# Neighbourhood pairs prepared between the key projections, their bias tables loaded, streamed weights placed 192 bytes in, and adaLN steps of the second layer run two at a time

## The chip, the cores and the metric

The kernel runs on one core of one Trainium2 chip. The metric is the device time of one execution in microseconds (us). Four compute engines work from queues of their own, in order: PE (TensorE: matmuls, and transposes done as matmuls), DVE (VectorE), ACT (ScalarE) and POOL (GpSimd). SP issues the loads of weights. Operands of a matmul lie in the on-chip buffer (SBUF, 128 partitions), results go to accumulators (PSUM).

## The reference

Two layers over 512 latent tokens and 256 context tokens of 1024 features, everything in fp32. Each layer has a mixer and a convolution feed-forward block (FFN), each behind an RMS norm that is modulated by a conditioning vector (adaLN).

- adaLN: `silu(c) @ ada_w[l] + ada_b[l]`, 1024 x 6144 for each layer, split in six vectors of 1024 (shift, scale and gate for the mixer and for the FFN).
- Layer 0 mixer: a bidirectional mLSTM with 4 heads and windowed attention with 8 heads.
- Layer 1 mixer: global attention with 8 heads over all 768 keys, and neighbourhood attention with 8 heads. The latent tokens form a grid of 8 rows and 64 columns; a query sees 16 columns of all 8 rows and the 256 context keys. To its scores on grid keys a bias is added that depends on the head and on the distance in rows and columns, `rpb[h, dr, dc]`, and -1e30 for columns out of reach. Then follow the softmax, the product with the values, and the output projection `x + gate * (mix @ w_out)`.
- FFN: `(silu(gate) * val) @ w_down`, where gate and val are `conv3(h @ w_up)`, 1024 to 5632 and 2816 to 1024.

## The kernel before

**Products.** Each fp32 operand is split into a high part and the rest (names end in hi and lo, or h and l), and each product is the sum of three matmuls: high with high, rest with high, high with rest. In `mm3` (L179) the weights are held in PE and the tokens stream; in `gemm_set` (L329) a tile of 128 tokens is held and 256 columns of weights stream. The normed tokens stand in `hlh`, `hll` (512 latent) and `hch`, `hcl` (256 context), made by `htiles` (L308), which starts `hch` and `hcl` 192 bytes further in than a round address, `hlh` and `hll` at one.

**Weights.** `wchunk` (L153) loads 512 KB from DRAM into one of four buffers `raw`, issued by SP; ACT copies the high part to `whi` (L160), POOL subtracts it to get `wlo` (L161), each with three buffers. `whi` and `wlo` start at a round address.

**adaLN.** The matrix of a layer goes in three rounds (`ada_round`, L192). A round has eight steps of 1 MB: two loads into `raw` (L198) and four matmuls of 32 x 512 (L201), one on each quarter of PE's columns. The first two rounds of layer 0 run beside the mLSTM (all of layer 0's second one between 197 and 235 us). The three rounds of layer 1 are spread over the first FFN: `wchunk` counts a pace (`WP`) for each chunk of weights and lets a step go where the count is full.

**Stages.** Layer 0's mixer and projection end near 450 us, the first FFN runs to 1062, layer 1's projections and global attention to 1270, neighbourhood attention and half of the output projection to 1378, the rest of it and the second FFN to the end.

**Neighbourhood attention.** Heads are taken in four pairs. `prepD` (L974) prepares one: transposes of keys and queries on PE (L557, in `stacks`), the splitting into `T` and `L` parts on ACT, DVE and POOL, moves by DMA, and a bias table `E` (L987): 128 query positions by seven blocks of 256, six of them computed from a row of `rpb` loaded by DMA and a column mask `cmask`, three by DVE and three by POOL, and one set to zero (L980). Each pair then has four query tiles. For a tile and each of its two heads there are two score matmuls (L1026) into an accumulator `s`, the bias added and the smallest taken by one DVE instruction (L1029; the scores are negated, so it is the greatest), the Exp on ACT (L586), the reciprocal of the sum on DVE (L587), the division on POOL (L588), then transposes (L604), copies (L607, L609) and the value matmuls (L624). The outputs of global attention are split into `hlh` by ACT (L1002) and `hll` by POOL (L1003), in code ahead of the first pair; half of the output projection (L1051, its residual input `xcq` and `xnq` read from DRAM) is laid among the pairs.

**Order.** A scheduler that runs with a model of the engines puts the instructions of each engine in order when the kernel is built. The order of the code sets the priority, `pvs` raises that of the value matmuls, and each tile tag has a fixed number of buffers, whose release later users wait for.

## Time and profile before

| | |
|---|---|
| median of 3 runs | 1781.68 us (1780.98 to 1784.17) |
| profiled execution | 1781.26 us |
| its span, first to last instruction | 1779.5 us |
| mean granted clock of PE | 0.989 |
| PE busy | 1700.4 us, 96% |
| DVE, ACT, POOL busy | 47%, 37%, 38% |
| DMA, mean | 105 GB/s |

A row of a group of instructions gives line, engine, operation, output and inputs, then count, busy time, mean duration in ns, and the idle time of the engine ahead of them. Matmul records overlap: the end of one is modelled, so the distance from one start to the next is the time that it takes in a row of its kind. An fp32 matmul of 512 columns in `ada_round` leaves two records.

### The profile page before, as it was taken

The page shows a single profiled execution, that of the slowest core. Times are in us where ns is not written, and L with a number is a line of the kernel's source. Part 1 is how long each engine was busy: PE and PEld are TensorE (multiplying, and loading weights), DVE is VectorE, ACT ScalarE, POOL GpSimd, SP SyncE. Part 2 cuts the span into 40 slices and gives each one's busy share as a digit, 9 for nine tenths or more (in the row PEclk, how much of TensorE's full clock was granted, in tenths as well). Part 3 has the DMA queues.
Part 4 walks back from the last instruction along what each step waited for, and adds up shares of the span by engine and source line. Part 5 has one row for each costly group of instructions (what it writes and reads, how often), then busy time and mean ns, then how long its engine had stood idle before and what let it go on. Part 6 is the DMA issues. An engine that isn't in the chain of part 4 may idle for free.

```text
span 1779.5 us, 27798 instructions
## 1 busy us (share of the span) xinstructions
PE 1700.4 (96%) x11057; PEld 1458.8 (82%) x11057; DVE 837.8 (47%) x1904; ACT 656.8 (37%) x1139; POOL 676.9 (38%) x539
## 2 busy tenths in 40 slices
PE   5899998899999999999999999899989899999999
PEld 5679788789878888888888888799867888888887
DVE  5642458776653321333134356866266643143242
ACT  4422333544443311322133343365544453242341
POOL 2133226434422222222322363634474443444442
PEclk9999999999999999999999999999999999999999
DMA  8442431411322333333431251311342422322322
GB/s 317 169 169 71 155 136 48 131 31 36 107 95 83 131 107 131 107 127 101 139 131 55 67 194 53 84 40 28 84 128 69 154 94 85 107 92 87 106 88 78
DMA packets 62257, 187.62 MB, mean 105 GB/s; under 512 B 8048, under 2 KB 14320, under 8 KB 61872
## 3 DMA queue, kind: packets, MB, share of 16 engines
q1 hardware_dynamic: 62128, 185.85, 31.9%
q8 instruction: 87, 1.43, 0.3%
q14 instruction: 42, 0.34, 0.1%
HBM read 170.68 MB, written 4.39 MB: 98 GB/s over the span
## 4 chain that ended last, share of the span: by engine, by line
PE 81%; DVE 8%; issue 3%; ACT 3%; DMA 2%; POOL 2%; SPq 0%; POOLq 0%; ACTq 0%; DVEq 0%
PE s L185 11%; PE s L189 11%; PE s L187 11%; PE mm L185 4%; PE mm L187 3%; PE mm L189 3%; PE o L624 3%; PE t L185 3%; PE t L189 3%; PE t L187 3%; PE t L604 3%; PE mm L336 2%; PE o L185 2%; PE o L187 2%; PE o L189 2%
## 5 line engine op out<-in xcount | busy, mean ns | idle before, releaser
L161 POOL TENSOR_TENSOR wlo<-raw,whi 128x1024 fp32r<-128x1024 f32 (+3 forms) x210 | 485.7, 2318 | 850.1 <-ACT whi L160 815.5
L160 ACT ACTIVATE whi<-raw 128x1024 fp32r<-128x1024 f32 (+3 forms) x210 | 214.9, 1027 | 507.2 <-PE s L187 176.9
L185 PE MATMUL s<-hlh,whi 128*128 128x512 f32 (+1 forms) x696 | 272.9, 392 | 1.6 <-DVE cv L1124 1.0
L189 PE MATMUL s<-hlh,wlo 128*128 128x512 f32 (+1 forms) x696 | 271.0, 389 | 1.7 <-POOL wlo L161 1.7
L187 PE MATMUL s<-hll,whi 128*128 128x512 f32 (+1 forms) x696 | 271.3, 390 | 0.0
L1123 DVE SCALAR_TENSOR_TENSOR cv<-s,convw,cv 128x511 f32<-128x511 f32 x125 | 82.1, 657 | 318.3 <-ACT cv L1117 318.2
L185 PEld LDWEIGHTS s<-hlh,whi 128*128 128x128 f32 x696 | 131.1, 188 | 42.6 <-issue 13.4
L189 PEld LDWEIGHTS s<-hlh,wlo 128*128 128x128 f32 x696 | 131.1, 188 | 29.4 <-POOL wlo L161 2.1
L187 PEld LDWEIGHTS s<-hll,whi 128*128 128x128 f32 x696 | 131.0, 188 | 26.2 <-issue 0.8
L588 POOL TENSOR_SCALAR P<-P,sm 128x512 f32<-128x512 f32 (+3 forms) x112 | 84.3, 756 | 109.5 <-DVE sm L587 81.3
L185 PE MATMUL s<-hch,whi 128*128 128x256 f32 x376 | 106.4, 283 | 0.0
L187 PE MATMUL s<-hcl,whi 128*128 128x256 f32 x376 | 106.2, 282 | 0.0
L189 PE MATMUL s<-hch,wlo 128*128 128x256 f32 x376 | 106.1, 282 | 0.0
L336 PE MATMUL mm<-whi,hlh 128*128 128x256 f32 x320 | 94.3, 295 | 6.1 <-ACT l1xt L898 2.4
L337 PE MATMUL mm<-wlo,hlh 128*128 128x256 f32 x320 | 92.0, 288 | 0.0
L338 PE MATMUL mm<-whi,hll 128*128 128x256 f32 x320 | 91.9, 287 | 0.1
L604 PE MATMUL t<-ident,P 128*128 128x128 f32 x496 | 77.8, 278 | 9.6 <-POOL E L987 4.8
L1124 DVE SCALAR_TENSOR_TENSOR cv<-s,convw,cv 128x511 f32<-128x511 f32 x125 | 82.5, 660 | 4.3
L185 PE MATMUL t<-gh,whi 128*128 128x512 f32 (+1 forms) x213 | 82.1, 386 | 0.0
L189 PE MATMUL t<-gh,wlo 128*128 128x512 f32 (+1 forms) x213 | 81.4, 382 | 0.0
L187 PE MATMUL t<-gl,whi 128*128 128x512 f32 (+1 forms) x213 | 81.0, 381 | 0.0
L1163 ACT ACTIVATE gh<-cv 128x768 fp32r<-128x768 f32 (+1 forms) x44 | 32.5, 739 | 122.7 <-DVE cv L1162 122.7
(460 smaller groups left out, 4078.5 us busy)
## 6 DMA issues: line engine op xcount, KB each, us to landing
raw<-ada SPq DMA_DIRECT2D x96, 512.0 KB, 4.0
raw<-up SPq DMA_DIRECT2D x86, 512.0 KB, 3.6
raw<-down SPq DMA_DIRECT2D x40, 448.0 KB, 3.2
raw<-wout SPq DMA_DIRECT2D x24, 512.0 KB, 3.5
raw<-wodd SPq DMA_DIRECT2D x18, 512.0 KB, 3.7
raw<-down SPq DMA_DIRECT2D x16, 512.0 KB, 3.5
raw<-wtok SPq DMA_DIRECT2D x12, 512.0 KB, 3.8
raw<-wqk SPq DMA_DIRECT2D x8, 512.0 KB, 4.1
```

Of the source, the lines that this page charges most:

```text
L160: nc.scalar.activation(hi[:, :cols], raw[:, :cols], AF.Copy)
L161: nc.gpsimd.tensor_tensor(lo[:, :cols], raw[:, :cols], hi[:, :cols], op=ALU.subtract)
L185: nc.tensor.matmul(ps, wh, hh(k), start=(k == 0), stop=False, skip_group_check=True)
L187: nc.tensor.matmul(ps, wh, hl(k), start=False, stop=False, skip_group_check=True)
L189: nc.tensor.matmul(ps, wl, hh(k), start=False, stop=(k == nk - 1), skip_group_check=True)
L336: nc.tensor.matmul(ps[:, :ncols], a, W[k][0], start=(k == 0), stop=False, skip_group_check=True)
L337: nc.tensor.matmul(ps[:, :ncols], a, W[k][1], start=False, stop=False, skip_group_check=True)
L338: nc.tensor.matmul(ps[:, :ncols], b, W[k][0], start=False, stop=(k == KT - 1), skip_group_check=True)
L588: nc.gpsimd.tensor_scalar(Pt[:, :n], Pt[:, :n], sm, 0.0, op0=ALU.mult, op1=ALU.add)
L604: nc.tensor.transpose(tp[:, (b - g0) * P:(b - g0 + 1) * P], Pts[e][:, b * P:(b + 1) * P], self.ident)
L1123: nc.vector.scalar_tensor_tensor(y[:, a + 1:b], u[:, 0:n - 1], w(0), y[:, a + 1:b], op0=ALU.mult, op1=ALU.add)
L1124: nc.vector.scalar_tensor_tensor(y[:, a:b - 1], u[:, 1:n], w(2), y[:, a:b - 1], op0=ALU.mult, op1=ALU.add)
```

## The change

1. `ada_round` takes `run`. The three rounds of layer 1 use `run=2`: a step has four loads, into four buffers of its own (`rawa`), and eight matmuls; the pace falls from 0.55 to 0.28. In every step the first matmul now waits for all loads of the step.
2. `chunks` asks `wchunk` for `whi` and `wlo` that start 48 floats (192 bytes) into a buffer of 1088. Weights for `mm3` stay at the start of theirs.
3. Pairs 0 and 1 are prepared between the two halves of the key and query projections; four buffers of `stacks` are handed out in the order T, L, T, L.
4. The bias tables are laid out on the host and loaded by one DMA of 917 KB for a pair, into two buffers. The 24 additions, four zeroings, eight loads of `rpb` and the load of `cmask` go.
5. Both heads of a query tile share one accumulator `s` (1024 columns). The scores keep their sign, so the greatest is taken and negated by an instruction of DVE of its own.
6. The splitting of global attention's outputs stands behind the first pair in the code.

```diff
-PACE1, PACE, WP = 2.2, 2.5, 0.55
+PACE1, PACE, WP = 2.2, 2.5, 0.28
+SKEW = 48, 64
...
-        new = keep or (lambda tag: self.stg.tile([P, 1024], F32R, tag=tag, bufs=WH, name=self.n(tag)))
+        new = keep or (lambda tag: self.stg.tile([P, 1024 + SKEW[1]], F32R, tag=tag, bufs=WH, name=self.n(tag))[:, skew:skew + 1024])
...
+        ks = max(run, 1)
+        for k0 in range(0, KT, ks):
+            loads = []
+            for k in range(k0, k0 + ks):
+                for h in range(2):
+                    raw = pool.tile([P, 1024], F32, tag="rawa", bufs=2 * ks, name=self.n("raw")) if run else self.raw()
...
+                    if i == 0 and q == 0:
+                        for *_, name in loads[1:]:
+                            self.tc.add_manual_dep(m.ins, name, AFTER)
+            if k0 + ks < KT:
...
-            hi, lo = self.wchunk(blk[:, k0:k1, :].rearrange("p k c -> p (k c)"), (k1 - k0) * ncols, keep)
+            hi, lo = self.wchunk(blk[:, k0:k1, :].rearrange("p k c -> p (k c)"), (k1 - k0) * ncols, keep, SKEW[0])
...
+        both = [new() for _ in range(4 if swapped else 2)]
+        T = both[::2] if swapped else both
...
+            E = ap.tile([P, 7, 256], F32, tag="E", bufs=2, name=self.n("E"))
+            nc.sync.dma_start(E, d["bias"][p])
...
+            if b == 0:
+                ready = [prepD(0), prepD(1)]
...
+            if 0 < p < 3:
+                ready.append(prepD(p + 1))
...
+                both = self.psum("s")
                 for e in range(2):
-                    s = self.psum("s")
+                    s = both[:, 512 * e:512 * e + 512]
...
-                                                   scale=1.0, scalar=3.0e38, op0=ALU.add, op1=ALU.min, accum_out=mx)
-                    self.probs(ap, S, S[:, 0:512], mx, 512, sign=-1.0)
+                                                   scale=1.0, scalar=-3.0e38, op0=ALU.add, op1=ALU.max, accum_out=mx)
+                    nc.vector.tensor_scalar(mx, mx, -1.0, None, op0=ALU.mult)
+                    self.probs(ap, S, S[:, 0:512], mx, 512)
...
+            if p == 0:
+                for pc in range(4):
+                    v = lambda m: m[:, pc, :].rearrange("p (r t c) -> p r t c", t=4, c=16)
+                    src = oC[:, pc].rearrange("p t (c r) -> p r t c", r=8)
+                    nc.scalar.activation(v(M[0]), src, AF.Copy)
+                    nc.gpsimd.tensor_tensor(v(M[1]), src, v(M[0]), op=ALU.subtract)
...
-    later = [self.ada_round(1, r, self.nrm) for r in range(3)]
+    later = [self.ada_round(1, r, self.nrm, run=2) for r in range(3)]
```

How it moves instructions shows in three places. The first is PE beside the mLSTM of layer 0, in its second adaLN round (L201, accumulator `mm`). Lines 454, 464, 473 and 475 are the mLSTM's. Before:

```order
L464 MATMUL t_1559<-qk 128x128
L201 MATMUL mm_2437<-raw_2460,sc 32x512 x2
L473 MATMUL s_1544<-V,W_1540 128x129
L475 MATMUL s_1544<-C_1482,qk 128x129
L464 MATMUL t_1582<-qk 128x128
L473 MATMUL s_1523<-V,W_1519 128x129
L475 MATMUL s_1523<-C_1482,qk 128x129
L464 MATMUL t_1605<-qk 128x128
L201 MATMUL mm_2437<-raw_2464,sc 32x512 x2
L337 MATMUL o_2484<-wlo_2456,hlh_87 128x256
```

and now (L210 is the matmul of adaLN, L466, L476, L485 and L487 the mLSTM's):

```order
L476 MATMUL t_1559<-qk 128x128
L485 MATMUL s_1544<-V,W_1540 128x129
L487 MATMUL s_1544<-C_1482,qk 128x129
L476 MATMUL t_1582<-qk 128x128
L485 MATMUL s_1523<-V,W_1519 128x129
L487 MATMUL s_1523<-C_1482,qk 128x129
L476 MATMUL t_1605<-qk 128x128
L210 MATMUL mm_2437<-raw_2460,sc 32x512 x2
L210 MATMUL mm_2437<-raw_2462,sc 32x512 x2
L485 MATMUL s_1544<-V,W_1540 128x129
```

The two pieces of two matmuls of a step have become one piece of four; over the whole round, 12 pieces (the first of eight matmuls) have become 7. In the first FFN, 24 pieces of four become 12 of eight, one of which stands in three parts.

The second place is POOL where neighbourhood attention begins: `hll` is the rest of global attention's outputs, `P` the probabilities, `wlo` weights, `E` the bias table. Before:

```order
L1003 TENSOR_TENSOR hll_12643<-cq,hlh_12642 128x512 x4
L588 TENSOR_SCALAR P_12705<-P_12705,sm_12707 128x512
L588 TENSOR_SCALAR P_12715<-P_12715,sm_12717 128x512
L588 TENSOR_SCALAR P_12739<-P_12739,sm_12741 128x512
L588 TENSOR_SCALAR P_12749<-P_12749,sm_12751 128x512
L161 TENSOR_TENSOR wlo_13516<-raw_13514,whi_13515 128x1024
L980 MEMSET E_12690 128x256
L987 TENSOR_TENSOR E_12690<-adab,raw_12689 128x256 x3
L980 MEMSET E_13124 128x256
L987 TENSOR_TENSOR E_13124<-adab,raw_13123 128x256 x3
L588 TENSOR_SCALAR P_12789<-P_12789,sm_12791 128x512
```

and now (L584 and L586 are the copies of `stacks`, L601 the division of `P`, L1045 `hll`, L163 `wlo`):

```order
L601 TENSOR_SCALAR P_12678<-P_12678,sm_12681 128x512
L601 TENSOR_SCALAR P_12688<-P_12688,sm_12691 128x512
L601 TENSOR_SCALAR P_12713<-P_12713,sm_12716 128x512
L601 TENSOR_SCALAR P_12723<-P_12723,sm_12726 128x512
L1045 TENSOR_TENSOR hll_12670<-cq,hlh_12669 128x512 x4
L601 TENSOR_SCALAR P_12764<-P_12764,sm_12767 128x512
L601 TENSOR_SCALAR P_12774<-P_12774,sm_12777 128x512
L601 TENSOR_SCALAR P_12799<-P_12799,sm_12802 128x512
L163 TENSOR_TENSOR wlo_13495<-raw_13493,whi_13494 128x1024
L163 TENSOR_TENSOR wlo_13529<-raw_13527,whi_13528 128x1024
L601 TENSOR_SCALAR P_12809<-P_12809,sm_12812 128x512
```

The four instructions for `hll` stand behind four for `P`, and none for `E` is left. The transposes of pairs 0 and 1 stay, on PE, where they were, near the end of global attention.

The third place is PE at the preparation of pair 3: the transposes from `nq` are the last that read it, and `xnq` is loaded over it. L604 are transposes of `P`, L1026 scores, L624 value matmuls. Before:

```order
L1026 MATMUL s_13229<-K_12872,Q_12892 128x512
L557 MATMUL t_13110<-ident,nq 128x128 x4
L604 MATMUL t_13156<-ident,P_13139 128x128 x4
L604 MATMUL t_13163<-ident,P_13149 128x128 x4
L604 MATMUL t_13190<-ident,P_13173 128x128 x4
L1026 MATMUL s_13253<-K_12871,Q_12889 128x512
L1026 MATMUL s_13253<-K_12871,Q_12891 128x512
L604 MATMUL t_13197<-ident,P_13183 128x128 x4
L1026 MATMUL s_13263<-K_12872,Q_12890 128x512
L1026 MATMUL s_13263<-K_12872,Q_12892 128x512
L624 MATMUL o_13134<-PT_13155,l1xt 64x128
```

and now (L570 the transposes of `stacks`, L1024 scores, L617 transposes of `P`, L187 to L191 the output projection):

```order
L570 MATMUL t_13090<-ident,nq 128x128 x4
L1024 MATMUL s_13227<-K_12856,Q_12874 128x512
L1024 MATMUL s_13227<-K_12856,Q_12875 128x512
L617 MATMUL t_13128<-ident,P_13110 128x128 x4
L617 MATMUL t_13135<-ident,P_13120 128x128 x4
L617 MATMUL t_13163<-ident,P_13145 128x128 x4
L1024 MATMUL s_13192<-K_12857,Q_12876 128x512
L1024 MATMUL s_13192<-K_12857,Q_12877 128x512
L1024 MATMUL s_13227<-K_12857,Q_12876 128x512
L1024 MATMUL s_13227<-K_12857,Q_12877 128x512
L187 MATMUL mm_13547<-hlh_12669,whi_13528 128x512
```

Sixteen transposes of `P`, four score matmuls and the 16 value matmuls of two tiles stood between the transposes from `nq` and the next product of the output projection; now it is twelve and six, and the value matmuls stand behind a product.

## Rows read from the trace of the kernel before

**Rows 1.** Stretches: length, busy time of PE, PEld, DVE, ACT, POOL, clock, DMA, GB/s.

```profile
0.00:20.00 20.00, 4.45 (x42) 3.45 (x42) 8.11 (x33) 10.49 (x20) 7.68 (x20) 1.00 0.88 320
200.00:240.00 40.00, 39.08 (x254) 26.50 (x253) 16.23 (x65) 12.73 (x39) 9.42 (x6) 1.00 0.72 250
520.00:1000.00 480.00, 480.00 (x2809) 405.24 (x2808) 153.21 (x236) 125.54 (x134) 129.28 (x55) 1.00 0.32 108
1280.00:1300.00 20.00, 15.92 (x103) 13.03 (x101) 11.04 (x18) 10.46 (x18) 17.19 (x18) 1.00 0.66 181
1300.00:1320.00 20.00, 17.25 (x96) 14.17 (x97) 13.28 (x32) 8.43 (x18) 14.39 (x14) 0.83 0.39 128
```

**Rows 2.** Timeline of PE, an adaLN step in the FFN: start, length, instruction.

```profile
576.94 1.06 PE L201 MATMUL o<-raw,sc 128*32 128x512 f32 x8
577.94 0.50 PE L185 MATMUL s<-hlh,whi 128*128 128x512 f32 x1
578.28 0.40 PE L187 MATMUL s<-hll,whi 128*128 128x512 f32 x1
578.51 0.39 PE L189 MATMUL s<-hlh,wlo 128*128 128x512 f32 x1
```

**Rows 3.** Timeline of PE, layer 0, two adaLN steps in one piece.

```profile
196.90 1.92 PE L201 MATMUL mm<-raw,sc 128*32 128x512 f32 x16
198.75 0.49 PE L454 MATMUL t<-V,kw 128*128 128x129 f32 x2
```

**Rows 4.** Stretches, line 201 alone: length, busy time of PE and PEld, clock, DMA, GB/s.

```profile
198.90:232.90 34.00, 11.56 (x40) 1.57 (x40) 1.00 0.74 256
520.00:1000.00 480.00, 23.44 (x176) 3.46 (x176) 1.00 0.32 108
```

**Rows 5.** Loads of adaLN: timeline of SP's queue, and issue to landing in us.

```profile
509.71 2.70 SPq L198 DMA_DIRECT2D raw<-ada  x2
raw<-ada SPq DMA_DIRECT2D x96, 512.0 KB, 4.0
```

**Rows 6.** Groups of PE by form, `gemm_set` with latent and context tokens held.

```profile
L337 PE MATMUL mm<-wlo,hlh 128*128 128x256 f32 x320 | 92.0, 288 | 0.0
L337 PE MATMUL mm<-wlo,hch 128*128 128x256 f32 x112 | 31.6, 282 | 0.0
```

**Rows 7.** Chain of waits at the start of global attention: start, length, what.

```profile
1149.19 3.58 DVE E L987 x3
```

**Rows 8.** Chain of waits at the start of neighbourhood attention; timeline of PE there.

```profile
1282.70 1.21 ACT hlh L1002
...
1284.04 6.38 POOL hll L1003 x4
1290.42 1.24 POOL P L588 x2
...
1293.11 2.36 POOL wlo L161
...
1295.72 3.12 POOL E L987 x3
...
1302.26 1.09 PE L604 MATMUL t<-ident,P 128*128 128x128 f32 x4 [4.77 <-POOL E L987]
```

**Rows 9.** Chain of waits behind the transposes of pair 3; timeline of PE there.

```profile
1343.00 6.18 DMA xnq<-xd
...
1349.20 0.76 DVE xnq L1070
...
1347.89 1.09 PE L624 MATMUL o<-PT,l1xt 128*64 128x128 f32 x16 [0.52 <-ACT PT L609]
...
1350.01 0.50 PE L185 MATMUL mm<-hlh,whi 128*128 128x512 f32 x1 [0.15 <-DVE xnq L1070]
```

**Rows 10.** A small instruction of DVE in neighbourhood attention.

```profile
L587 DVE RECIPROCAL sm<-sm 128x1 f32<-128x1 f32 x32 | 5.1, 160 | 9.4 <-ACT P L586 9.2
```

More of the change, by code (lines that the diff above doesn't have):

```diff
@@ L550, in stacks @@
         new = lambda: pool.tile([P, n], F32R, tag=tag, bufs=bufs, name=self.n(tag))
-        T = [new(), new()]
-        L = [new(), new()] if swapped else [pool.tile([P, TOK], F32R, tag="stL", bufs=1, name=self.n("stL"))[:, :n]] * 2
+        both = [new() for _ in range(4 if swapped else 2)]
+        T = both[::2] if swapped else both
+        L = both[1::2] if swapped else [pool.tile([P, TOK], F32R, tag="stL", bufs=1, name=self.n("stL"))[:, :n]] * 2
         for g0 in range(0, nt, 4):
@@ L972, in odd_mixer @@
             self.qk_norm(ap, nq[:, :, c], NLT, 4, None, None, tmp)
-        def prepD(p):
-            ks = self.stacks(ap, nk, p * P, NTT, "K", False, bufs=4, g=nag[:, 1:2])
-            qs = self.stacks(ap, nq, p * P, NLT, "Q", True, bufs=8, rev=True, g=nag[:, 0:1])
-            raw = self.raw()
-            E = (self.res.tile([P, 8, 256], F32, tag=("hch", "hcl")[p // 2], name=self.n("E")) if p % 2 else
-                 ap.tile([P, 7, 256], F32, tag="E", bufs=1, name=self.n("E")))
-            nc.gpsimd.memset(E[:, 3], 0.0)
-            for e in range(2):
-                h = 2 * p + e
-                R = raw[:, e * 512:e * 512 + 265]
-                nc.sync.dma_start(R, bass.AP(tensor=rpb.tensor, offset=rpb.offset + 64 + h * 465 - 16, ap=[[1, 16], [31, 8], [1, 265]]))
-                for v in range(3):
-                    view = bass.AP(tensor=R.tensor, offset=R.offset + 16 - 8 * v, ap=[R.ap[0], [1, 32], [31, 8]])
-                    (nc.vector, nc.gpsimd)[e].tensor_tensor(E[:, 4 * e + v].rearrange("p (c r) -> p c r", r=8),
-                                                            cmask[:, v].unsqueeze(2).to_broadcast([P, 32, 8]), view, op=ALU.subtract)
-            return ks, qs, E
+            if b == 0:
+                ready = [prepD(0), prepD(1)]
         self.pve = 1
-        nxt = prepD(0)
         for b in range(2):
@@ L1300, in layout @@
     a["cos1"], a["sin1"] = tl(np.cos(ang)[cols]), tl((np.sin(ang) * sgn)[cols])
-    cq = (P - 1 - np.arange(P)) // 8
-    mask = []
-    for i, c0 in ((0, 0), (1, 8), (3, 32)):
-        ck = c0 + np.arange(32)
-        st = np.clip(16 * i + cq - 8, 0, 48)[:, None]
-        mask.append(np.where((ck >= st) & (ck < st + 16), 0.0, -NEG))
-    a["cmask"] = C(np.stack(mask, 1).astype(f))
+    q = P - 1 - np.arange(P)
+    rows = np.arange(8)[None, None, :] - (q % 8)[:, None, None] + 7
+    tabs = np.zeros((4, P, 7, 256), f)
+    for v, (i, c0) in enumerate(((0, 0), (1, 8), (3, 32))):
+        cq, ck = (16 * i + q // 8)[:, None, None], (c0 + np.arange(32))[None, :, None]
+        st = np.clip(cq - 8, 0, 48)
+        seen = (ck >= st) & (ck < st + 16)
+        idx = rows * 31 + np.clip(ck - cq + 15, 0, 30)
+        for h in range(8):
+            tabs[h // 2, :, 4 * (h % 2) + v] = np.where(seen, g["na_rpb"][0, h].reshape(-1)[idx], f(NEG)).reshape(P, 256)
+    a["bias"] = tabs
     for k, s in _SHAPES.items():
```

43 lines of the change are left out of this document (17 added, 26 removed).

## The prediction

> **What bounds the kernel now.** I read the stretches first. In the first FFN PE is busy for all of its 480 us at full clock, with DMA at 32% [rows 1]: there, only fewer or shorter instructions of PE save time, and any wait put on PE costs its full length. The second adaLN round of layer 0 is mixed, PE 39.08 of 40 us and DMA at 72% [rows 1]. Where neighbourhood attention starts (1280 to 1320) PE is idle for 4.08 + 2.75 us, and in the second half the granted clock is 0.83 [rows 1]. If the time below full clock was spent at 1.2 GHz, the lower of its two levels, 0.17 x 20 us = 3.4 us of work were lost to it too: some 10 us in all. Then the chain of waits, for what stands behind that idle time: it runs through ACT and POOL, `hlh`, `hll`, two `P`, a `wlo`, then the bias tables [rows 8]. Last, the timelines of PE around single adaLN steps, for the price of a step.
>
> **The sum, part by part.** It is made against the profiled execution, 1781.26 us (its span 1779.5 and 1.8 around it), which lies 0.4 us below the median of the runs.
>
> *adaLN in the first FFN.* One step of four matmuls takes 577.94 - 576.94 = 1.00 us, and the next matmul then takes 0.34 to the start of the one behind it, where the following one takes 0.23: 0.11 more [rows 2]. Two steps in one piece took 198.75 - 196.90 = 1.85 us [rows 3]. Twice 1.11 against 1.85 + 0.11 saves 0.26 a pair. Of the 12 pairs one stands in three parts, so 11 x 0.26 = -2.9 us. If only the 0.11 is saved, it is -1.2; if the trace's first piece hides some more, -4. The new wait of a piece's first matmul for four loads I cost at nothing: the stretch moves 108 GB/s [rows 1], a piece comes once in some 480 / 12 = 40 us, its four buffers are its own and free as soon as the piece before is done, and a load lands 4.0 us after its issue [rows 5]. What it costs without that cover is the third rival.
>
> *adaLN in layer 0.* After the first piece, 40 records, that is 20 matmuls in pieces of one or two, kept PE 11.56 us [rows 4]. Five steps in pieces of four cost 5 x 1.06 = 5.3 by the length of the step of [rows 2]: -6.3 us if PE alone sets the pace. But each piece now waits for both of its loads, and the round reads its megabytes through the four buffers that the other weights use too, at 256 GB/s [rows 4]; the highest rate that a row shows is 320 [rows 1]. The 12 adaLN loads and 3 of weights of that stretch are 7.9 MB, 25 us at that rate, of 34: loads can follow PE only in part. So 0 to -6.3, and I take the middle, -3.
>
> *Weights 192 bytes in.* In `gemm_set` the weights stand at a round address. With `hlh` held, at a round address too, the mean record is 288 ns; with `hch` held, which starts 192 bytes in, 282 [rows 6]. After the change the pairs are swapped: weights and latent tokens lie differently, weights and context tokens alike. If that is what makes the 6 ns, the 1392 matmuls with `hlh` or `hll` win and the 528 with `hch` or `hcl` lose (both counted over all groups of lines 336 to 338, of which [rows 6] show one each). Records overlap, a start following the last by 0.12 us, so I take 6/288 of 0.12, 2.5 ns each: 2.5 x (1392 - 528) = -2.2 us. Ends: 0, and with the whole 6 ns, -5.2.
>
> Against this part stands a rule of the Trainium skill, "TensorE: Matmul & The Clock Gate", in "Step-by-step: what each phase is for": PE reads the streamed operand and the next held operand through two independent ports, and "Loading the next tile's weights doesn't steal SBUF read bandwidth from the running matmul". By that rule the distance between two operands would not matter and the term would be 0. The rows with 288 and 282 ns speak against it, though weakly, as the ends of matmul records are modelled.
>
> *Bias tables.* At the start of global attention DVE spends 3.58 us on three of them in the chain of waits [rows 7], while score work waits behind it. It goes. Half of it will be lost to the next late thing, DVE's own queue of norms: -1.8, between 0 and -3.6. The loads of 0.9 MB that replace it go in stretches where DMA has room (66% at most, [rows 1]).
>
> *Start of neighbourhood attention.* Three things go from POOL's queue before the `P` that PE waits for: two memsets with their additions, 3.12 us for three [rows 8], and the four `hll`, 6.38 us [rows 8], which now stand behind the first four `P`. The 4.77 us that PE waited for the table [rows 8] goes, and the late first `P` (at 1290.42) comes some 6 us earlier. What is late next is the fifth `P`, behind `hll`; by then PE has the transposes, value matmuls and projections of two query tiles. Of the 10 us I count -8.
>
> Two things come back. Behind the transposes of pair 3, `xnq` is loaded in 6.18 us, and the product that needs it started 0.15 us after its release [rows 9]: before, the 16 value matmuls (1347.89 to 1350.01, 2.1 us) were part of its cover. They now stand behind that product, so PE waits for about 2 us more: +2. And DVE gets 32 negations of one column. The nearest row is the reciprocal of a column, 160 ns [rows 10]: 5.1 us of DVE in all, each between the maximum and the Exp. With two heads in flight most of it lies beside other work; I take +1, between 0 and +5.1. The shared accumulator `s` changes which scores may run ahead, not their number: 0, between -1 and +1. Together -8 + 2 + 1 = -5, between -10 and +1.
>
> That pairs 0 and 1 are prepared earlier in the code I cost at nothing: the order leaves their transposes where they were on PE.
>
> Sum: -2.9 - 3 - 2.2 - 1.8 - 5 = -14.9, so 1766.4 against the profiled execution, and 1767 with the 0.4 to the median.
>
> **The rivals.**
>
> *The gain at neighbourhood attention is given back.* The first `P` is early, but the negations sit in every chain from score to Exp, `hll` is late for the first product of the projection, and the wait for `xnq` drops the clock as the wait at 1302 did. Then the -5 becomes 0: 1772. For it speaks that PE's idle time between 1280 and 1380 has many releasers, so that removing one shows the next; against it, that POOL held 17.19 of 20 us there [rows 1] and loses 6 of them.
>
> *The offset does nothing*, by the skill's rule above or because the 6 ns belongs to the tokens alone. All else as forecast: 1769.
>
> *Slower: each piece of eight waits for its loads.* PE takes its queue in order, so a piece whose fourth load has not landed holds the whole FFN. SP issues four loads in a row behind weight loads, which wait for a buffer that POOL releases; two adaLN loads took its queue 2.70 us [rows 5]. One such time late at each of 12 pieces is 12 x 2.7 = +32, against -15: 1799. It decides from 15 / 12 = 1.2 us late a piece. Against it: in the order SP's four loads stand ahead of weights that PE uses after the piece, and the stretch leaves two thirds of DMA idle.
>
> *Nothing that counts.* The layer 0 round stays with its loads, the start of neighbourhood attention is set by ACT's Exps, pieces of eight save 1.2: 1779 or so.
>
> **How the numbers follow.** The forecast 45%, with a range of its own of 1760 to 1771; the gain given back 22%; no effect of the offset 13%; the slower one 10%; nothing that counts 10%. A measurement of this kernel tells some 0.2%, 3.6 us, from no change. Faster by more than that are the first three, 80%; within it the last and a weak form of the slower one, 11%; slower 9%. All ends of the terms at once would give 1781.3 - 4 - 6.3 - 5.2 - 3.6 - 10 = 1752, or 1781; half way to the first, and past no change at the other end, the range is 1757 to 1781, which leaves out the slower rival and a little below.
>
> **What would show it.** In the FFN, 12 pieces of 16 records with 1.85 us to the next start and no idle time ahead of them, PE still busy for all of 520 to 1000; a bracket with a DMA as releaser at those pieces proves the third rival. Between 199 and 235, six pieces of 8 records of about 1.06 us, and weight matmuls some 3 us earlier from there on; idle time of PE released by `raw<-ada` means the loads set the pace. The mean record of line 348 to 350 falls with `hlh` and rises with `hch`; if all stay, the offset does nothing. At the start of neighbourhood attention, no bracket of 4.77 us and a granted clock of 1.00; if PE waits for ACT's Exp or for `hll` by as much, the first rival holds. Behind pair 3's transposes, a wait for `xnq` of about 2 us.

## The result and the profile after

The changed kernel takes 1771.34 us (median of 6 runs, 1767.76 to 1775.91) against 1781.87 us of the kernel before (6 runs, 1780.06 to 1786.64): ratio 0.9939, 95% interval 0.9925 to 0.9952. It is faster, by 0.6% or 10.9 us; 1767 was forecast, with a range of 1757 to 1781. The profiled execution took 1767.76 us, with a span of 1766.0.

The runs of the changed kernel differ by 8 us (13 in one of the kernels below), and their mean granted clock differs with them (0.982 to 0.990 in the changed kernel). One of the twelve runs of skew_alone, below, was slow, at 3768.69 us, and is left out of its ratio. Two measures stand beside the ratio. One is where a given matmul starts in two traces. Of each kernel there is one trace, and kernels with the same code differ in it: by up to 4.9 us at the end of layer 0's second adaLN round, by about 1 us in how long the first FFN takes. The other is span times mean granted clock, averaged over the runs of a kernel: an estimate of the time at full clock. Its standard deviation over the runs of one kernel is 1 to 3 us, so that two means of six runs that are less than some 3 us apart can't be told apart by it.

Where the 13.5 us between the two traces come from (start of the same matmul, read from both traces):

| | before | after | difference |
|---|---|---|---|
| first matmul of `gemm_set`, behind the first adaLN round of layer 0 | 117.3 | 113.3 | -4.0 |
| first value matmul of windowed attention, behind the second round | 337.8 | 330.7 | -7.1 |
| first product of the first FFN | 486.5 | 479.0 | -7.5 |
| first projection of layer 1 | 1061.7 | 1054.6 | -7.1 |
| first score of global attention | 1138.3 | 1129.7 | -8.5 |
| last score of neighbourhood attention | 1368.8 | 1354.7 | -14.1 |
| first product of the second FFN | 1420.8 | 1408.4 | -12.4 |
| end of PE | 1776.3 | 1762.8 | -13.5 |

**adaLN.** The stretches of line 210 alone, as in [rows 4] (length, busy time of PE and of weight loads, clock, DMA, GB/s), of the changed kernel:

```profile
50.00:120.00 70.00, 8.33 (x64) 1.45 (x64) 0.98 0.58 192
195.00:231.00 36.00, 6.39 (x48) 0.97 (x48) 1.00 0.73 253
520.00:1000.00 480.00, 22.41 (x176) 4.62 (x176) 1.00 0.32 108
```

Between 195 and 231, 24 matmuls take 6.39 us where 20 took 11.56 [rows 4]: a piece of four takes 1.00 us to the start of what follows, where a piece of two or of one took 0.98. (The trace of the kernel before has 13 pieces in the second round, two of them of one matmul.) Over that round this is 7.9 us of pieces for 13.6. But PE now waits more among them. The round as a whole, all instructions, before and after (columns as in [rows 1]):

```profile
190.00:240.00 50.00, 48.92 (x334) 34.49 (x333) 21.26 (x84) 14.48 (x46) 10.90 (x7) 1.00 0.60 205
```

```profile
190.00:240.00 50.00, 45.69 (x362) 36.65 (x362) 26.06 (x79) 15.97 (x45) 15.70 (x9) 1.00 0.66 224
```

and PE's longest waits in it (who waits for whom: us in total, times, longest), before and after:

```profile
PE o L336 <- ACT whi L160: 0.8, 1, 0.8
```

```profile
PE o L348 <- DVE bq L760: 2.4, 1, 2.4
PE o L348 <- ACT whi L162: 1.1, 1, 1.1
```

Part of the matmul time that was saved has turned into waits for DVE and ACT (`bq` is a copy that frees an accumulator).

The FFN has 22.41 us for the same 176 records that took 23.44 [rows 4]. The timeline of PE in the first FFN (start, length, instruction, idle time before and its releaser), with the first piece and the wait that follows later:

```profile
484.02 1.92 PE L210 MATMUL o<-raw,sc 128*32 128x512 f32 x16
485.88 0.50 PE L187 MATMUL mm<-hlh,whi 128*128 128x512 f32 x1
...
510.99 0.77 PE L187 MATMUL s<-hlh,whi 128*128 128x512 f32 x1 [2.06 <-DVE cv L1129]
511.55 0.63 PE L189 MATMUL s<-hll,whi 128*128 128x512 f32 x1
511.98 0.63 PE L191 MATMUL s<-hlh,wlo 128*128 128x512 f32 x1
```

A piece of eight takes 1.86 us, as forecast, and none waits for its loads. But 25 us later PE waits 2.06 us for DVE, and the matmuls behind the wait take 0.56 and then 0.43 us to the next start instead of 0.23. The stretch it stands in (columns as in [rows 1]), changed kernel:

```profile
510.00:520.00 10.00, 9.01 (x40) 7.66 (x41) 5.04 (x8) 1.98 (x3) 0.00 (x0) 0.83 0.06 22
```

The granted clock is 0.83 there: it fell to 1.2 GHz behind the wait, which costs 0.17 x 10 = 1.7 us. The kernel before had a step of four just ahead of that place, a wait of 0.95 behind it, and no loss of clock:

```profile
515.54 1.19 PE L201 MATMUL o<-raw,sc 128*32 128x512 f32 x8
517.68 0.47 PE L185 MATMUL s<-hlh,whi 128*128 128x512 f32 x1 [0.95 <-DVE cv L1124]
```

```profile
510.00:520.00 10.00, 9.04 (x54) 7.13 (x53) 8.08 (x13) 6.00 (x7) 4.41 (x2) 1.00 0.65 225
```

**Streamed weights.** Rows of `gemm_set` in the changed kernel, to be held against [rows 6]:

```profile
L349 PE MATMUL mm<-wlo,hlh 128*128 128x256 f32 x320 | 91.1, 285 | 0.0
...
L349 PE MATMUL mm<-wlo,hch 128*128 128x256 f32 x112 | 31.9, 285 | 0.0
```

288 fell to 285 with latent tokens held and 282 rose to 285 with context tokens held. From one start to the next, over all pairs of neighbours without idle time between, the distance went from 119.5 to 115.6 ns (latent) and from 116.9 to 119.4 ns (context). The 115.6 is a mean of two spacings: of 1194 intervals 637 are 113 to 115 ns and 520 are 116 to 119, and a chunk of weights, twelve matmuls in a row, mostly has the one or the other. Two sets of twelve intervals (timeline of PE, first and last start), 1.36 us and 1.41:

```profile
113.33 0.28 PE L348 MATMUL t<-whi,hlh 128*128 128x256 f32 x1
...
114.69 0.28 PE L348 MATMUL t<-whi,hlh 128*128 128x256 f32 x1
```

```profile
1094.12 0.28 PE L348 MATMUL t<-whi,hlh 128*128 128x256 f32 x1
...
1095.53 0.28 PE L348 MATMUL t<-whi,hlh 128*128 128x256 f32 x1
```

So the offset of 192 bytes does not decide alone. The buffers of 1088 floats follow each other at 4352 bytes, 17 times 256, so that chunks with the same offset within 256 bytes can differ within 512; whether that makes the two spacings was not tested.

**Global attention.** The stretch in which DVE had computed bias tables, before and after:

```profile
1140.00:1160.00 20.00, 16.77 (x123) 15.08 (x122) 19.49 (x36) 9.94 (x23) 15.97 (x25) 1.00 0.30 81
```

```profile
1140.00:1160.00 20.00, 19.44 (x183) 18.45 (x180) 19.23 (x49) 14.16 (x33) 10.83 (x11) 1.00 0.17 54
```

PE is busy 2.7 us longer of the 20. Of the score matmuls, the one at 1152 of the kernel before comes 8.3 us earlier now, the one at 1160 comes 11.0 us earlier.

**Neighbourhood attention.** Two stretches of the changed kernel, then POOL's timeline at its start:

```profile
1240.00:1280.00 40.00, 35.95 (x321) 33.12 (x318) 10.70 (x28) 15.21 (x31) 12.65 (x14) 0.96 0.32 83
1280.00:1320.00 40.00, 39.50 (x296) 33.33 (x296) 21.88 (x70) 22.93 (x46) 26.57 (x24) 1.00 0.51 155
```

```profile
1267.42 0.69 POOL L601 TENSOR_SCALAR P<-P,sm 128x512 f32<-128x512 f32 x1 [3.23 <-DVE sm L600]
1271.20 1.40 POOL L601 TENSOR_SCALAR P<-P,sm 128x512 f32<-128x512 f32 x2 [3.08 <-DVE sm L600]
1274.54 0.70 POOL L601 TENSOR_SCALAR P<-P,sm 128x512 f32<-128x512 f32 x1 [1.95 <-DVE sm L600]
1279.70 6.45 POOL L1045 TENSOR_TENSOR hll<-cq,hlh 128x512 fp32r<-128x512 f32 x4 [4.46 <-ACT hlh L1044]
1286.07 0.75 POOL L601 TENSOR_SCALAR P<-P,sm 128x512 f32<-128x512 f32 x1
```

The first `P` comes at 1267, 23 us earlier than at 1290.42 [rows 8] where the trace as a whole is 8 to 14 earlier; POOL waits for DVE and not PE for POOL. The 4.77 us wait [rows 8] is gone, and 1280 to 1320 runs at full clock. What is late next stands at its very start, in the stretch with the clock at 0.96: PE waits for a move of `Q`:

```profile
1264.62 0.73 PE L1024 MATMUL s<-K,Q 128*128 128x512 f32 x2 [2.46 <-DMA Q<-Q]
```

The product behind pair 3, on PE and on DVE:

```profile
1328.00 0.73 PE L1024 MATMUL s<-K,Q 128*128 128x512 f32 x2
1330.24 0.73 PE L1024 MATMUL s<-K,Q 128*128 128x512 f32 x2 [1.51 <-DVE mx L1027]
1330.90 0.50 PE L187 MATMUL mm<-hlh,whi 128*128 128x512 f32 x1
```

```profile
1330.10 0.75 DVE L1075 SCALAR_TENSOR_TENSOR xnq<-mm,mod,xnq 128x512 f32<-128x512 f32 x1
```

The product starts at 1330.90, 0.05 us after DVE is done with `xnq`, as before the change. The idle time of 1.51 us just ahead of the last two scores was ended by DVE's `mx`, which frees the accumulator that they need. A DVE row shows what the negations cost (count, busy time, mean ns):

```profile
L1029 DVE TENSOR_SCALAR mx<-mx 128x1 f32<-128x1 f32 x32 | 4.4, 150 | 0.2
```

Behind neighbourhood attention 1.7 us are given back (-14.1 to -12.4 in the table). There PE waits for DVE's `x`, the output of the projection, ahead of the second FFN, before and after:

```profile
1398.63 0.38 PE L185 MATMUL t<-hlh,whi 128*128 128x256 f32 x1 [1.06 <-DVE x L1070]
```

```profile
1385.10 0.58 PE L187 MATMUL t<-hlh,whi 128*128 128x256 f32 x1 [2.44 <-DVE x L1075]
```

and the granted clock of 1380 to 1390 is 0.83 in the changed kernel, while it is 1.00 over 1370 to 1430 in the kernel before.

### The profile page after: what moved, and what is told of

It reads as the page before. It is cut to its first block, busy times and chain, and to the rows that moved or that the text cites. A ratio compares the mean times of both kernels' runs of the same rounds, so it can differ in the third digit from the quotient of the medians.

```text
span 1766.0 us, 27837 instructions
## 1 busy us (share of the span) xinstructions
PE 1683.0 (95%) x11057; PEld 1453.7 (82%) x11057; DVE 830.0 (47%) x1924; ACT 655.5 (37%) x1139; POOL 663.6 (38%) x523
## 5 line engine op out<-in xcount | busy, mean ns | idle before, releaser
L163 POOL TENSOR_TENSOR wlo<-raw,whi 128x1024 fp32r<-128x1024 f32 (+3 forms) x210 | 486.7, 2323 | 827.2 <-ACT whi L162 768.7
L187 PE MATMUL s<-hlh,whi 128*128 128x512 f32 (+1 forms) x696 | 272.4, 391 | 2.8 <-DVE cv L1129 2.2
L191 PE MATMUL s<-hlh,wlo 128*128 128x512 f32 (+1 forms) x696 | 271.1, 389 | 1.7 <-POOL wlo L163 1.7
L187 PEld LDWEIGHTS s<-hlh,whi 128*128 128x128 f32 x696 | 131.1, 188 | 38.4 <-ACT whi L162 7.3
L191 PEld LDWEIGHTS s<-hlh,wlo 128*128 128x128 f32 x696 | 131.1, 188 | 30.9 <-POOL wlo L163 2.2
L601 POOL TENSOR_SCALAR P<-P,sm 128x512 f32<-128x512 f32 (+3 forms) x112 | 83.0, 742 | 126.7 <-DVE sm L600 95.4
L187 PE MATMUL s<-hch,whi 128*128 128x256 f32 x376 | 106.4, 283 | 0.0
L191 PE MATMUL s<-hch,wlo 128*128 128x256 f32 x376 | 106.2, 282 | 0.0
L187 PE MATMUL t<-gh,whi 128*128 128x512 f32 (+1 forms) x213 | 81.7, 384 | 0.0
L617 PE MATMUL t<-ident,P 128*128 128x128 f32 x496 | 76.3, 276 | 5.4 <-POOL P L601 2.2
L191 PE MATMUL t<-gh,wlo 128*128 128x512 f32 (+1 forms) x213 | 81.2, 381 | 0.0
```

The costliest lines, as they stand in the source:

```text
L163: nc.gpsimd.tensor_tensor(lo[:, :cols], raw[:, :cols], hi[:, :cols], op=ALU.subtract)
L187: nc.tensor.matmul(ps, wh, hh(k), start=(k == 0), stop=False, skip_group_check=True)
L191: nc.tensor.matmul(ps, wl, hh(k), start=False, stop=(k == nk - 1), skip_group_check=True)
L601: nc.gpsimd.tensor_scalar(Pt[:, :n], Pt[:, :n], sm, 0.0, op0=ALU.mult, op1=ALU.add)
L617: nc.tensor.transpose(tp[:, (b - g0) * P:(b - g0 + 1) * P], Pts[e][:, b * P:(b + 1) * P], self.ident)
```

## The experiments

Each kernel was timed together with the kernel before, on one chip; the groups ran on different chips, and the changed kernel was timed in a group of its own. So a difference to the changed kernel in medians is one between groups, and the difference of the ratios to the kernel before is the safer one. "At full clock" is the estimate defined above; it is 1760 for the kernel before (1760.1 over 23 runs, 1759.2 to 1759.9 in the later groups) and 1745.3 for the changed kernel. Differences in it are against the kernel before of the same group, unless the changed kernel is named.

**skew_alone**, the kernel before with part 2:

```diff
+        new = keep or (lambda tag: self.stg.tile([P, 1024 + SKEW[1]], F32R, tag=tag, bufs=WH, name=self.n(tag))[:, skew:skew + 1024])
+            hi, lo = self.wchunk(blk[:, k0:k1, :].rearrange("p k c -> p (k c)"), (k1 - k0) * ncols, keep, SKEW[0])
```

> The kernel before with part 2 alone: the streamed weights of gemm_set start 192 bytes in; the order of every engine is that of before. Theory (the distance between the two operands' start addresses sets the spacing): from one matmul's start to the next, those with hlh or hll held fall from 119.5 to about 115.6 ns as in the changed kernel, those with hch or hcl rise from 116.9 to about 119.5; 1392 x -3.9 + 528 x +2.5 ns = -4.1 us, so about 1777.5. Rival (two independent read ports, so the offset does nothing and the changed spacing comes from other shifts of addresses): 119.5 and 116.9 stay, 1781.5.

1778.37 us, ratio 0.9985 (0.9974 to 0.9997); at full clock -2.5. The spacings came as the theory said: 115.1 ns with `hlh` or `hll`, 119.5 with `hch` or `hcl`. Of the 4.1 us that this makes, 2.5 reach the end; the rest stands in stretches where PE waits anyway (in the trace the kernel is 1 us ahead at 290 us and behind again at 333). The run also has the build setting `dynamic_dma_scratch_size=1024` of the changed kernel; skew_undone has it too.

**skew_undone**, the changed kernel with part 2 taken back:

```diff
-SKEW = 48, 64
+SKEW = 0, 64
```

> The changed kernel with part 2 alone undone: weights at the start of their wider buffers, every engine's order that of the changed kernel. Theory: hlh 115.6 back to 119.5 ns, hch 119.5 back to 116.9, +4.1 us against the changed kernel, a span of about 1770 where the profile of the changed kernel had 1766. Rival: spacing and span stay.

1774.70 us, ratio 0.9958 (0.9945 to 0.9972), 3.4 us more than the changed kernel; at full clock 2.2 more, which by itself can't be told from nothing. 119.5 and 117.0 ns are back. Two sets of the same 21 intervals show it (timeline of PE, first and last start): the changed kernel

```profile
1071.53 0.29 PE L350 MATMUL t<-whi,hll 128*128 128x256 f32 x1
...
1073.92 0.28 PE L350 MATMUL t<-whi,hll 128*128 128x256 f32 x1
```

and skew_undone

```profile
1073.30 0.28 PE L350 MATMUL t<-whi,hll 128*128 128x256 f32 x1
...
1075.81 0.28 PE L350 MATMUL t<-whi,hll 128*128 128x256 f32 x1
```

2.39 us against 2.51 (the first set lies in chunks with the shorter spacing). In both pairs of kernels the order of every engine is the same row by row, so only the offset differs. The Trainium skill's rule of two independent read ports ("TensorE: Matmul & The Clock Gate", "Step-by-step: what each phase is for") would make the offset worth nothing; the measured 119.5 and 115.6 ns, with nothing but the offset changed, say otherwise here.

**ada_alone**, the kernel before with part 1 (its core):

```diff
+                    if i == 0 and q == 0:
+                        for *_, name in loads[1:]:
+                            self.tc.add_manual_dep(m.ins, name, AFTER)
...
+        later = [self.ada_round(1, r, self.nrm, run=2) for r in range(3)]
```

> The kernel before with part 1 alone (pieces of four that wait for their loads, pieces of eight and pace 0.28 in the first FFN). Theory (the two rounds of layer 0 gain by pieces that stay together, the FFN nothing): about -3 us by 137 us, about -4 more by 290, 0 in the FFN because the steps that go from its start were filling a wait for DVE there; -5 to -7, so about 1776. Rival A (layer 0's early gain comes from the weights' offset): by 137 us not more than -1. Rival B (the FFN gains its 2 to 3 us, and the loss at its start comes from other parts): 1773.

1779.34 us, ratio 0.9981 (0.9970 to 0.9993). The trace follows the theory: -3.7 at 117 us, -8.2 at 275, -7.5 behind the FFN. At full clock it is -8.0. But the mean granted clock of its 12 runs is 0.9858, where the kernel before has 0.9884: 0.0026 x 1780 = 4.6 us are lost again. The trace shows two places: behind the wait at 511 (2.05 us), and behind the wait for `x` ahead of the second FFN (2.44 us, where the lead over the kernel before shrinks from 7.8 to 5.2 us); each costs 1.7 us of clock. Rival A falls (the first round gains without the offset), rival B too.

**pairs_alone**, the kernel before with parts 3 to 6 (its core):

```diff
+            nc.sync.dma_start(E, d["bias"][p])
...
+                ready = [prepD(0), prepD(1)]
...
+                both = self.psum("s")
```

> The kernel before with parts 3 to 6 alone (early preparation, loaded tables, shared accumulator, later split). Theory: unchanged up to 1060 us; about -2.7 at the start of global attention, where the tables leave DVE's queue, -4 more to the end of neighbourhood attention, +2 behind it, because the projection ends with less cover; about -5, 1777. Rival (the loss behind neighbourhood attention belongs to another part): -7, 1775.

1776.05 us, ratio 0.9967 (0.9955 to 0.9979); at full clock -4.9, with a mean clock of 0.9892. In the trace PE's start moves by -2.2 where the tables left DVE (1137 to 1157) and by about -4 more to the end of neighbourhood attention; nothing is lost behind it. From 1062 to the end it is -6.6, as its rival said; the loss behind neighbourhood attention stands in ada_alone and not here. The three parts alone add up to -15.4 at full clock, the whole change has -14.8.

**ffn_old**, the changed kernel with the FFN's rounds as before:

```diff
-PACE1, PACE, WP = 2.2, 2.5, 0.28
+PACE1, PACE, WP = 2.2, 2.5, 0.55
-        later = [self.ada_round(1, r, self.nrm, run=2) for r in range(3)]
+        later = [self.ada_round(1, r, self.nrm) for r in range(3)]
```

> The changed kernel with the three rounds of layer 1 in steps of four matmuls at pace 0.55 as before; layer 0's pieces as in the changed kernel. Theory (in the FFN the part is worth nothing: 2.2 us saved by pieces of eight, as much lost at its start): the same, within 1 us, with the wait at 511 as before (0.95) and 1.00 as the clock of 510 to 520. Prediction: 2.9 us slower.

1772.32 us, ratio 0.9937 (0.9918 to 0.9955): the time of the changed kernel, within what can be told. In the trace the FFN changes by +0.2 us (2.8 behind at 444, 3.0 at 1046). At 511 it has no wait of 2.06 us, but one of 0.40 and one of 0.60, and the clock stays at 1.00. At full clock it is 2.3 more than the changed kernel, and its mean clock is higher, 0.9872 for 0.9862. That fits pieces of eight that save work which the clock takes back, but neither difference is clear of the spread of the runs.

**layer0_old**, the changed kernel without the wait for both loads in layer 0:

```diff
-                    if i == 0 and q == 0:
+                    if run and i == 0 and q == 0:
```

> The changed kernel without the wait of a step's first matmul for both loads in layer 0, so that the steps there fall in pieces as before; the FFN as changed. Theory (both rounds of layer 0 gain, 3.7 and 4.4 us): +8 us at 290 us, about 1778 to 1779 at the end, less what the clock gives back. Prediction: +3 us, all of it between 197 and 235, 1774.

1777.37 us, ratio 0.9964 (0.9951 to 0.9978), 6.0 us more than the changed kernel (4.5 by the ratios, 6.6 at full clock). Its trace is +3.7 at 113 us, +7.6 at 297. The rows of line 210 show both rounds in their old pieces (compare the first row of the changed kernel above):

```profile
50.00:120.00 70.00, 10.66 (x64) 2.03 (x64) 0.95 0.55 183
190.00:240.00 50.00, 14.55 (x64) 2.15 (x64) 1.00 0.61 205
```

Against all traces the step is smaller than against the changed kernel's, which is the fastest of its kind here: at 290 us the four traces with the old pieces stand 7.8 to 8.6 us behind it, the ten with the new pieces 0 to 4.9, on average 2.0. So the pieces of layer 0 are worth some 6 us there. At full clock this one line is the largest single part of the change.

**ffn_filler**, the changed kernel with the FFN's pieces moved to where PE waits:

```diff
+                self.lastmm = nc.tensor.matmul(ps, wl, hh(k), start=False, stop=(k == nk - 1), skip_group_check=True).ins.name
...
+                    if run and i == 0 and q == 0:
+                        self.tc.add_manual_dep(m.ins, self.lastmm, ORDER)
...
                     self.work, self.pace = work
+                    self.due = 0.75
```

> The changed kernel with the adaLN pieces of the first FFN tied to the end of the product before them and counted from 0.75, so that the first one stands where PE waited 2.06 us for DVE at 511 (it stood at 484, with no wait behind it). Theory (in the changed kernel, steps that had filled this wait went elsewhere, and the longer wait takes the clock down there): the wait shrinks to about 0.2, the granted clock of 510 to 520 is 1.00 instead of 0.83, about -3.5 us against the changed kernel; 1767 to 1768 as median. Rival (the wait is the same length wherever the pieces stand, because DVE is behind anyway, and the lower clock comes from elsewhere): as the changed kernel, 1771.

1767.77 us, ratio 0.9908 (0.9895 to 0.9922), 3.6 us less than the changed kernel (5.5 by the ratios). The place of the wait, and its stretch, in this run:

```profile
511.81 0.47 PE L187 MATMUL s<-hlh,whi 128*128 128x512 f32 x1 [0.21 <-DVE cv L1131]
```

```profile
510.00:520.00 10.00, 9.79 (x63) 7.54 (x56) 5.87 (x10) 2.81 (x4) 0.00 (x0) 1.00 0.72 255
```

The wait is 0.21 us and the clock 1.00. In the trace the FFN is 3.6 us shorter (1.4 behind at 444, 2.2 ahead at 1046). The rival falls: what stands ahead of the wait decides its cost.

**s_apart**, the changed kernel with an accumulator for each head:

```diff
-                both = self.psum("s")
...
-                    s = both[:, 512 * e:512 * e + 512]
+                    s = self.psum("s")
```

> The changed kernel with an accumulator of its own for each head's scores, as before; tables loaded, early preparation and the negations stay. Theory (what neighbourhood attention gained came from the tables that left DVE and POOL; the shared accumulator is worth nothing): within 2 us of the changed kernel, 1771, and at the end of neighbourhood attention (1363 in the changed kernel's profile) within 2 us too. Rival (scores of both heads in one accumulator let PE run ahead, and that made the gain): 3 to 6 us slower, lost between 1261 and 1363.

1769.04 us, ratio 0.9918 (0.9900 to 0.9936), not slower than the changed kernel; its trace goes from 4.4 us behind at 1046 to 1.9 at 1361. (Most of the 4.4 come from layer 0's second round, where its order is that of the changed kernel, but the clock 0.90 and not 1.00, in the row below.) The shared accumulator gains nothing, and may cost 2 us, which these intervals can't tell. That leaves the loaded tables (part 4) as the likely cause of the gain in neighbourhood attention; no run undoes them alone. Parts 3 and 6 were not run apart either; that moving them back leaves every engine's order as it is, so that they are worth nothing, is not shown by a trace here.

```profile
190.00:240.00 50.00, 46.09 (x329) 36.12 (x328) 24.33 (x75) 14.65 (x42) 13.12 (x8) 0.90 0.62 206
```

**skew_96**, the changed kernel with another offset, and **skew_two**, ffn_filler with one for each layer:

```diff
-SKEW = 48, 64
+SKEW = 24, 64
```

```diff
-            hi, lo = self.wchunk(blk[:, k0:k1, :].rearrange("p k c -> p (k c)"), (k1 - k0) * ncols, keep, SKEW[0])
+            hi, lo = self.wchunk(blk[:, k0:k1, :].rearrange("p k c -> p (k c)"), (k1 - k0) * ncols, keep, self.shift)
...
+    shift = 16
...
+        self.shift = 32
```

> The changed kernel with the streamed weights 96 bytes in instead of 192, every engine's order the same. Theory (equal start offsets are slow, different ones fast): latent tokens at 0 and context tokens at 192 both differ from 96, so hlh stays at 115 to 117 ns and hch falls from 119.5 to 115 to 117; 528 x -3 ns = -1.6 us. Rival (only 192 bytes, or a distance near it, is fast): both near 119.5, +5 us of work.

> The kernel of run ffn_filler with the streamed weights 64 bytes in for layer 0 and 128 bytes in for layer 1. 96 bytes were as slow as 0 for latent tokens (119.6 ns) and half way for context tokens (118.0), so being different isn't enough. Theory (the distance has to be a multiple of 64 bytes and not of 256): layer 0 with latent tokens (distance 64) and context tokens (128 less), layer 1 with latent (128) and context (64 less) all at 115 to 117 ns; 528 x -3 ns against 192 bytes, -1.6 us of work. Rival (192 bytes has something of its own, 64 to 256 bytes round the other way): distances of 128 stay at 119.5, +1 to +3 us.

1773.50 us (0.9944, 0.9932 to 0.9956) and 1768.31 us (0.9918, 0.9900 to 0.9935). At 96 bytes the latent tokens are as slow as at 0 (119.8 ns) and the context tokens in between (118.0), so the theory of skew_96 falls. skew_two has 117.2 and 118.7 in layer 0, 118.7 and 115.3 in layer 1. Taken as start of the streamed operand less that of the held one, round 256 bytes, the means of the runs agree: 0 gives 119.5, 64 117.2, 96 119.8, 128 118.7, 160 118, 192 115.5. 64 and 192 are faster, 128 isn't: the theory of skew_two was half right.

**skew_all** and **skew_shared**, ffn_filler with other offsets for all operands:

skew_all puts context tokens at 0 and the weights of `mm3` 64 bytes in (the same edit for `wqk` and `wout`):

```diff
-        skew(48)
-        skew(16)
-            hi, lo = self.wchunk(w[:, c:c + n], n, keep)
+            hi, lo = self.wchunk(w[:, c:c + n], n, keep, 16)
```

skew_shared keeps that offset of the weights, and has besides:

```diff
-SKEW = 48, 64
+SKEW = 0, 64
...
+        skew(16)
         lat = tile("hlh", LAT), tile("hll", LAT)
...
-        skew(16)
```

> The kernel of run ffn_filler with every distance (start of the streamed operand less start of the held one, round 256 bytes) set to 192 where the tokens are one of the two: context tokens start at 0, the weights held in mm3 (all but those of the down projection) 64 bytes in, the streamed weights 192 bytes in as in the changed kernel. Theory (spacing follows this distance: 0 119.5 ns, 64 117.2, 96 119.8, 128 118.7, 160 118, 192 115.5 in the runs so far): gemm_set with context tokens 119.4 to 115.5 (528 x -4 ns = -2 us); the 2457 matmuls of 512 columns with latent tokens streamed, at distance 0 now, 227 to about 223 ns (-10 us); 1757 as median. Rival (the table holds for 256 columns and held tokens alone; the products of gh and gl, 512 columns at distances 64 and 128, show 230 to 231): 227 rises to 230, +7 us, 1773; the -2 us of gemm_set stays.

> The kernel of run ffn_filler with latent tokens and the weights held in mm3 64 bytes in, context tokens and the streamed weights of gemm_set at 0; every engine's order the same. So 2457 matmuls of 512 columns stay at distance 0 (as fast as a run has shown them, 227 ns; 233 at 192), the 1479 of 256 columns with context tokens come to 192 with both starts as in run skew_all (114 to 115 ns there, 118 in ffn_filler), gemm_set has 192 with latent and 0 with context tokens as in the changed kernel. Theory (the distance alone decides, by the number of columns): 227 stays, 118 to about 114.5, 115.5 and 119.4 stay; 1479 x -3.4 ns = -5 us, 1763 as median. Rival (the place of each operand counts too, not the distance alone): 512 columns rise above 229 or gemm_set loses its 115.5, and nothing is gained.

skew_all took 1772.65 us (0.9946, 0.9933 to 0.9960), as its rival said. The rows of `mm3` in the FFN, with 512 and with 256 columns, of ffn_filler and of skew_all:

```profile
L187 PE MATMUL s<-hlh,whi 128*128 128x512 f32 x688 | 270.1, 393 | 0.8 <-ACT whi L162 0.4 <-ACT zs L387 0.2 <-DVE cv L1131 0.2
...
L187 PE MATMUL s<-hch,whi 128*128 128x256 f32 x376 | 106.4, 283 | 0.0
```

```profile
L187 PE MATMUL s<-hlh,whi 128*128 128x512 f32 x688 | 273.7, 398 | 0.9 <-ACT whi L162 0.4 <-DVE cv L1129 0.3 <-ACT zs L385 0.2
...
L187 PE MATMUL s<-hch,whi 128*128 128x256 f32 x376 | 104.8, 279 | 0.0
```

From start to start 512 columns went from 227 to 233 ns, 256 columns from about 118 to 114.5, and `gemm_set` to 114.8 with context tokens. skew_shared took 1763.36 us (0.9897, 0.9878 to 0.9916), the number that was expected, but not for the expected reason: its 512 columns stay at 227, and the 256 columns stay at 117.5 to 118, where 114.5 was expected; `gemm_set` with latent tokens, at 192 again, has 116.1. At full clock it equals ffn_filler (1742.7 and 1742.5); its mean clock was higher, 0.9892 for 0.9870. So the distance round 256 bytes alone doesn't decide in `mm3`, the rival holds, and the two kernels can't be told apart by their intervals. Both beat the kernel before and the changed one.

## Why the prediction was right, and where not

- **The sum.** -14.9 was forecast. At full clock it came out at -14.8 (-13.9 against the later groups of the kernel before); 10.9 arrived. The 3 to 4 us between are clock: 0.9862 as mean of the runs, where the kernel before has 0.9884 over 23 runs (0.0022 x 1780 = 3.9; 0.9873 to 0.9884 by group). The prediction counted lost clock at one place that the change mends and nowhere as a thing that the change might cause. That is the step that failed, and it made the likeliest time 4 us too short: 1771.34 lies just above the forecast's own range of 1760 to 1771. The traces show three places where it is lost: behind the wait of 2.05 to 2.07 us at the start of the first FFN (1.7 us); in layer 0's second round, where the clock fell in five of the ten traces with the new pieces (1.7 us, in s_apart 5.1, with 0.90 as clock of 190 to 240) and in none of the four with the old ones; and behind the wait for `x` ahead of the second FFN (2.15 to 2.44 us in eight traces, seven of which lose 1.7 us or more between 1370 and 1430; of the six with 1.46 us or less one does).
- **Luck.** That the sum at full clock agrees is in part luck: layer 0 gave 3 to 5 us more than its term, the first FFN 3 less, the start of neighbourhood attention 1 to 2 less.
- **adaLN in layer 0: -3 forecast, -6 to -8 measured** (at full clock 6.6 by layer0_old and -8.0 by ada_alone; in the traces 6.2 on average, with 7.6 and 8.2 for these two). In the changed kernel's trace the second round gave -4.4, between its ends of 0 and -6.3. What kept it from the latter was not the loads but DVE and ACT: PE's waits between 190 and 240 rose from 1.0 to 1.6 us in the four traces with old pieces to 2.9 to 5.5 in the ten with new ones, with `bq`, `num` and `whi` as releasers (`raw<-ada` in skew_undone alone, 0.46 and 0.33 us). The first round gave -3.7, and the prediction had no term for it: the order showed pieces of 8, 8, 5, 3, 4, 2, 2 there and 8, 4, 4, 4, 4, 4, 4 now. Line 201 took 10.69 us of PE with the old pieces, 8.33 is taken with the new; from start to start the pieces take 10.2 and 9.4. A wait of 1.2 us for DVE's `adasb` (the copy of the round's sums) at the end of the round has gone too (1.3 in layer0_old, none in ada_alone).
- **adaLN in the first FFN: -2.9 forecast, nothing measured.** The size of the saving was about right on PE (23.44 to 22.41 in the same stretch, and less to wait behind fewer pieces), but a step had been filling a wait for DVE at the FFN's start. Moved ahead, it left 2.06 us of idle time and the clock at 0.83; ffn_filler gets 3.6 us back.
- **Weights 192 bytes in: -2.2 forecast, -2.5 and -2.2 measured**, the second within the spread of the runs. That the offset sets the spacing is shown by skew_alone and skew_undone; what about the offset does it is open. The spacing changed by more than forecast (-3.9 ns for -2.5), and part of it was lost to waits.
- **Bias tables: -1.8 forecast, -2.2 to -2.7 measured**, at the place that was named.
- **Start of neighbourhood attention: -5 forecast, about -3 to -4 measured.** The 4.77 us wait and the loss of clock at 1300 went. The +2 behind pair 3 came as 1.51 + 0.46 + 0.35 us at 1324 to 1331, with DVE and POOL as releasers, not `xnq`; `xnq`, done 0.05 us ahead of the product, would have held it to about the same time. The negations take 4.4 us of DVE; what they cost was not measured apart. What I had not named is the wait for a move of `Q` at 1264 (2.46 us).
- **The rivals.** The third (pieces wait for loads) did not happen: no piece of the changed kernel's trace has a DMA as releaser. The second (the offset does nothing) is refuted. The first named neighbourhood attention as the place where the gain is given back, and 1772 as the time: the time is right and the place is wrong, since pairs_alone gains 0.33%. The fourth (nothing that counts, 1779) falls with the interval of the ratio.
- **Open.** Which of the other short waits in layer 1 (1100, 1260, 1330) take the clock down varies from trace to trace, also in the kernel before, and was not settled. Why 256 columns reach 114.5 ns in skew_all and not in skew_shared, with the same distance, is open too, and so are the two spacings of `gemm_set` at one offset.

## What to carry to other kernels

Where PE takes its queue in order and short groups of matmuls on a quarter of its columns are interleaved with others, bind each group together, even at the price of a wait for its loads: here a group of two cost almost as much as one of four. Before moving work away from a stretch, see whether it stands ahead of a wait: there it is free, and the wait that it leaves can cost clock as well. Add the granted clock of every run to the comparison; here it hid 3 to 4 of some 15 us. And compare more than one trace: the changed kernel's own was the fastest of ten at 290 us, and alone it made the gain of layer 0 look 2 us larger.

## What the runs showed of the hardware

- The mean spacing of matmuls of 256 columns changed with nothing but the start address of the streamed operand: 115.6 to 119.5 ns with latent tokens held in the changed kernel and skew_undone, 114.8 to 119.8 over all runs and both kinds of tokens. Behind such a mean can stand two spacings (113 to 115 and 116 to 119 ns) at one offset within 256 bytes. For 512 columns the cheap distance is another one: 227 ns at 0 and 233 at 192, by ffn_filler and skew_all.
- The wait for DVE at the start of the first FFN is 2.05 to 2.07 us in six traces (changed kernel, skew_undone, ada_alone, skew_96, s_apart, layer0_old), and the granted clock over the 20 us around it is 0.91 in each. In the other eight the waits there are at most 1.05 us, and it is 1.00 in each. The length of a wait does not tell it everywhere: in layer 0's second round the changed kernel, skew_undone, ada_alone and skew_two wait 2.34 to 2.40 us with 1.00 as clock of 190 to 240.
